# A hybrid attention layer on one core: keys and values projected second, the remaining projections run between attention units

## The chip, the cores and the metric

The kernel runs on one core of one Trainium2 chip. The metric is device time in microseconds (us) of one execution, the median over the runs. A core has TensorE (PE, matmuls into the PSUM banks; its weight loads are shown apart), VectorE (DVE), ScalarE (ACT), GpSimd (POOL) and SyncE (SP), which only issues DMAs here. Each engine works through its own instructions in order; semaphores tie them together.

## The reference

One layer of a backbone with 128 prompt tokens (tile t = 0) and 1024 latent tokens (t = 1 to 8), width 1024. All is fp32.

```
h = rmsnorm(x) * (1 + scale) + shift            # shift, scale, gate = silu(c) @ w_mod + b_mod
q_a k_a v_a g_a q_b k_b v_b g_b = split(h @ w_in)   # 8 query heads of 64, 2 key heads, for A and for B
q, k = rmsnorm per head; latent ones with 2-D axial rotation
A: softmax over all 1024 latent keys + 128 cached keys
B: softmax over keys with |i-j| <= 128 + 128 cached keys + a sink logit per head
y = x + gate * (concat(o_a * silu(g_a), o_b * silu(g_b)) @ w_out)
```

Prompt tokens attend to prompt keys alone. The outputs are y for both kinds of tokens, and the prompt's keys and values of A and B.

## The kernel before, in words

A product in fp32 is made of three matmuls: both operands are split into a high and a low part (fp32r), and high x high, high x low and low x high are added in PSUM. So the projection of one tile of 128 tokens onto 512 columns is 8 k-tiles x 3 = 24 matmuls of 512 columns (`project`, L247 to L251), and the gates, which are made transposed, are 24 matmuls a piece of 512, 256 or 384 columns (`gate_products`, L253 to L264). `Weights.split` makes the parts of one raw weight tile: a cast on ACT, a subtraction on DVE (for `gb`, every other one on POOL).

The program is one long list, written in the order in which each engine is to run it. `later(n, f)` puts work `n` ticks ahead; a tick comes every 12 projection matmuls, later once per attention slot. At the end `in_order` pins every engine to this order.

Before, the stages follow each other: modulation and mixer A's gates (W_GA), A's queries (W_QA, 9 tiles), B's queries (W_QB, 9 tiles), keys and values (W_KV, 9 tiles), B's gates (W_GB), then attention with the output projection.

- `query`: a projected query tile is squared on ACT, reduced on DVE, raised to -1/2 on POOL, scaled and rotated on DVE, transposed on TensorE, split into high (ACT) and low (DVE), and put into DRAM (`q_dram`). `u_load` brings it back for each unit.
- `key`: the same for keys, which stay in SBUF: `kha`, `kla` for A, `khb`, `klb` for B; values in `v_hi`, `v_lo`.
- A unit is (tile t, mixer m, key head g). An A unit has 9 key blocks, a B unit 3 or 4; a slot is one block. `scores` makes a block's scores in a B-bank; for A `exp` (L1123) and a cast (L1127) on ACT and a subtraction on POOL (L1131, the fifth block of a unit on DVE, L1129) give the high and low parts, for B the weights are normalised ahead and the block is a transpose, a cast (L1116) and a subtraction on DVE (L1117). `values` multiplies with the values LAG slots later (LAG = 3).
- Ahead of an A unit `max_items` makes row maxima (12 matmuls of 384 columns, L881, each with a reduction on DVE, L882), and a product into the tile `qb` (L901). Ahead of a B unit `weight_items` makes scores row by row (L938, L939), a masked reduction (L942), an exponential (L928) and the sums. Both use the two A-banks.
- At a unit's end `inverse`, `gated` and `parts` divide by the sums, multiply with the stored gates on POOL, and split into `ogh` (ACT, L1177) and `ogl` (POOL, L1179).
- `out_items`: 24 output matmuls (L1212) for each half of a tile go into `outq`; the slot loop takes OUTRATE of them per slot. `split_wo` splits the output weights in the places that the projections' inputs leave free.

Units alternate, A, B, A, B of each tile; the prompt's four units come last.

```
units = [(t, m, g) for t in range(1, NT) for g in range(2) for m in range(2)]
units[PROMPT_AT:PROMPT_AT] = [(0, m, g) for g in range(2) for m in range(2)]
```

The maxima of the first two A units are now made between B's gate matmuls (`EARLY`).

## Time and profile before

| | us |
|---|---|
| median of 3 runs (lowest to highest) | 711.58 (711.53 to 712.5) |
| profiled execution, first to last instruction | 709.6 |
| of it TensorE busy | 691.6 |
| DVE, ACT, POOL busy | 469.3, 409.9, 334.2 |

Stages by TensorE: gates of A done at 82.5, A's queries to 133.9, B's queries to 191.4, keys to 247.2, B's gates to 303.2, attention to 688.0, and the last output matmuls and sums to 709.6. The profiled execution's span stands 2.0 us under the median of the runs. TensorE's busy time is modelled for pipelined matmuls, so that two matmuls overlap in it; the distance between their starts tells more. A row of the groups gives line, engine, operation, output and input tiles, shapes, count, then busy us and mean ns of one, then the engine's idle time before them and what ended it.

### The profile page before, as it was taken

What the parts mean: (1) busy time and instruction counts of PE and PEld (TensorE: products, weight loads), DVE (VectorE), ACT (ScalarE), POOL (GpSimd) and SP (SyncE); (2) the same over time, 40 slices, a digit from 0 to 9 for tenths busy, and PEclk for the clock granted to TensorE, in tenths of its full rate; (3) what the DMA queues carried; (4) which work ended last, traced back from release to release, by engine and by line L of the source; (5) the groups of instructions that cost most, each with busy time, mean ns of one, the idle gap of its engine ahead of it and who ended that gap; (6) DMA issues with size and microseconds to landing.
All of it is one profiled execution on the core that took longest, in us unless ns stands there. A gap on an engine that the chain in (4) does not pass through costs nothing. (4 is left out here: it accounts for less than half of the span.)

```text
span 709.6 us, 10604 instructions
## 1 busy us (share of the span) xinstructions
PE 691.6 (97%) x3508; PEld 558.5 (79%) x3508; DVE 469.3 (66%) x1019; ACT 409.9 (58%) x829; POOL 334.2 (47%) x356
## 2 busy tenths in 40 slices
PE   7999999999999999989999999999999999999987
PEld 4778988878787889966788888888888888787865
DVE  4667257967848945647867578666775776675662
ACT  5646412412403431188777887787778777877760
POOL 3547023233213421256756655665576557555660
PEclk9999999999999999999999999999999999999999
DMA  8962283358353116332222121212221221222323
GB/s 316 415 211 102 78 302 74 90 154 263 84 139 104 37 39 215 123 108 57 78 68 85 50 82 53 71 57 75 68 82 38 79 71 50 78 72 70 104 67 121
DMA packets 53560, 78.58 MB, mean 111 GB/s; under 512 B 7096, under 2 KB 25720, under 8 KB 52608
## 3 DMA queue, kind: packets, MB, share of 16 engines
q1 hardware_dynamic: 45328, 65.96, 28.1%
q10 hardware_dynamic: 8176, 11.94, 6.3%
q8 instruction: 28, 0.46, 0.3%
q14 instruction: 28, 0.23, 0.1%
HBM read 58.69 MB, written 19.18 MB: 110 GB/s over the span
## 5 line engine op out<-in xcount | busy, mean ns | idle before, releaser
L1131 POOL TENSOR_TENSOR pl<-pe,ph 128x512 fp32r<-128x512 f32 x130 | 167.7, 1292 | 145.0 <-DVE nm L942 67.5
L882 DVE TENSOR_REDUCE mx<-pmx 128x1 f32<-128x384 f32 x192 | 101.4, 552 | 56.3 <-PE pmx L881 54.8
L1123 ACT ACTIVATE pe<-st 128x512 f32<-128x512 f32 x146 | 86.8, 594 | 28.2 <-PE st L1121 27.4
L1127 ACT CAST ph<-pe 128x512 fp32r<-128x512 f32 x146 | 90.6, 621 | 4.8
L1141 PE MATMUL pv<-ph,v_hi 128*128 128x512 f32 x208 | 82.8, 398 | 2.2 <-DVE spare L1165 2.2
L1144 PE MATMUL pv<-pl,v_hi 128*128 128x512 f32 x208 | 82.4, 396 | 0.0
L1212 PE MATMUL po<-wo,ogh 128*128 128x512 f32 x216 | 72.6, 395 | 0.2 <-DVE yt L1219 0.2
L174 POOL TENSOR_TENSOR rs_q<-ms_q,mhalf 128x8 f32<-128x8 f32 x18 | 34.1, 1896 | 80.9 <-DVE ms_q L172 80.9
L942 DVE CUSTOM_DVE_ANT_0 sn<-sn,mask,nsink 128x512 f32<-128x512 f32 (+1 forms) x64 | 46.4, 724 | 38.0 <-PE sn L939 37.6
L881 PE MATMUL pmx<-kha,qt 128*128 128x384 f32 x192 | 61.2, 363 | 0.4 <-ACT pen L928 0.2
L1120 PE MATMUL st<-qt,kha 128*128 128x512 f32 x144 | 58.2, 404 | 1.9 <-ACT pe L1123 1.1
L1121 PE MATMUL st<-qb,kla 68*128 68x512 f32 x144 | 57.5, 399 | 1.1 <-DVE qb L901 1.1
L1143 PE MATMUL pv<-ph,v_lo 128*64 128x512 f32 x146 | 57.6, 395 | 0.0
L1144 PEld LDWEIGHTS pv<-pl,v_hi 128*128 128x128 f32 x208 | 39.2, 189 | 16.4
L928 ACT ACTIVATE pen<-sn,nm 128x512 f32<-128x512 f32 (+2 forms) x72 | 45.0, 626 | 6.5 <-DVE nm L942 3.1
L1116 ACT CAST ph<-st 128x512 fp32r<-128x512 f32 x62 | 36.4, 587 | 19.9 <-PE st L1115 18.7
L1141 PEld LDWEIGHTS pv<-ph,v_hi 128*128 128x128 f32 x208 | 39.3, 189 | 10.6 <-ACT ogh L1177 2.4
L646 ACT CAST qo0q<-ptq 128x512 fp32r<-128x512 f32 x18 | 10.6, 586 | 60.7 <-PE ptq L643 55.8
L1212 PEld LDWEIGHTS po<-wo,ogh 128*128 128x128 f32 x216 | 40.0, 188 | 6.8 <-DVE yt L1219 0.6
L1117 DVE TENSOR_TENSOR pl<-st,ph 128x512 fp32r<-128x512 f32 x62 | 42.5, 686 | 2.7 <-ACT ph L1116 2.1
L1212 PE MATMUL po<-wo,ogl 128*128 128x512 f32 x108 | 42.6, 394 | 0.0
L881 PEld LDWEIGHTS pmx<-kha,qt 128*128 128x128 f32 x192 | 35.6, 191 | 6.4 <-DVE mx L882 1.3
(213 smaller groups left out, 1699.2 us busy)
## 6 DMA issues: line engine op xcount, KB each, us to landing
qt<-qd SPq DMA_DIRECT2D x36, 256.0 KB, 3.0
wm<-in_w_mod_ss_dram SPq DMA_DIRECT2D x7, 1024.0 KB, 10.0
qd<-qo0q ACTq DMA_DIRECT2D x36, 128.0 KB, 2.4
qd<-qo1q ACTq DMA_DIRECT2D x36, 128.0 KB, 2.4
sgl<-gd SPq DMA_DIRECT2D x36, 128.0 KB, 2.2
out_dram<-yt SPq DMA_DIRECT2D x17, 256.0 KB, 2.0
xn<-in_x_sample_dram SPq DMA_DIRECT2D x8, 512.0 KB, 7.2
wg<-in_w_mod_g_dram SPq DMA_DIRECT2D x4, 1024.0 KB, 8.3
```

The lines of the kernel that those rows point to most:

```text
L881: nc.tensor.matmul(pm[:, 0:384], lhs, kha[:, g, 3 * b : 3 * b + 3, :], start=True, stop=True)
L882: nc.vector.tensor_reduce(mx[:, h, b : b + 1], pm[:, 0:384], axis=AX.X, op=ALU.max)
L942: nc.vector.tensor_tensor_reduce(s, s, mask[:, m0 : m0 + n], -1.0, nsink[:, 4 * g + h : 4 * g + h + 1], op0=ALU.add, op1=ALU.min, accum_ou ...
L1120: nc.tensor.matmul(s, kh, qtile[i], start=True, stop=False)
L1121: nc.tensor.matmul(s, kl, qbtile[i], start=False, stop=True)
L1123: nc.scalar.activation(pe, s, AF.Exp)
L1127: nc.scalar.copy(ph, pe)
L1131: nc.gpsimd.tensor_tensor(pl, pe, ph, op=ALU.subtract)
L1141: nc.tensor.matmul(pv, two, ph, start=(b == 0), stop=False)
L1143: nc.tensor.matmul(pv[0:64, :], vl, ph, start=False, stop=False)
L1144: nc.tensor.matmul(pv, two, pl, start=False, stop=last)
L1212: nc.tensor.matmul(po[n], a, wo_parts[KT * n + k][lo], start=(k == KS[0] and p == 0), stop=(k == KS[-1] and p == 2))
```

## The change

The stages are put in another order. Behind A's gates come keys and values; behind them the first five tiles of A's queries; then attention begins. The other 13 query tiles and all of B's gates become a list `light` of single matmuls, which the slot loop takes from at LIGHT = 6 columns-of-512 per slot between a unit's own matmuls, while eleven A units run (t = 1 to 5, and the first of t = 6). B units and the output projection begin after them.

```
FIRST_UNITS = [(t, 0, g) for t in range(1, 6) for g in range(2)] + [(6, 0, 0)]
REST = """B1.0 B1.1 A6.1 B2.0 B2.1 A7.0 B3.0 B3.1 A7.1 B4.0 B4.1 A8.0 B5.0 B5.1 A8.1 B6.0 B6.1
 B7.0 B7.1 A0.0 A0.1 B8.0 B0.0 B0.1 B8.1"""
OUT_ORDER = (1, 2, 3, 4, 5, 6, 7, 0, 8)
```

To make room, B's keys and values are put into DRAM when they are made and loaded later, and the gated outputs of A units of t = 1 to 8 are put into DRAM and fetched, one half at a time, when their tile's output is due. Fewer buffers stand between the steps: LAG 3 to 2, NOG 5 to 4, PES 3 to 2, and one `desk` for the query steps. Query parts are put by SP instead of ACT once attention runs; B's gates are made without `Silu` (as x times exp(-ln(1 + exp(-x)))), so that ACT keeps its set of functions.

```diff
-LAG = 3
+LAG = 2
-NOG = 5
-PES = 3
+NOG = 4
+PES = 2
-OUTRATE = 2.5
-PADRATE = 3
+LIGHT = 6.0
+OUTRATE = 3.9
+SOON = 5
+MX_LEAD = 9
+NAT_LEAD = 7
...
+        order = list(range(1, NT)) + [0]
+        for m, (w, nxt) in enumerate(((W_QA, W_QB), (W_QB, W_GB))):
+            for t in order:
+                items = project_items(w, nxt, m, t, t == order[-1])
+                if t == order[-2]:
+                    items.insert(0, (0.0, nxt.load_all))
+                light += items
...
+        light.append((0.0, lambda: later(1 + QUERY_SLOT[-1] + 2, queries_done)))
+        for a, b in THIRDS:
+            for ch in range(4):
+                light += piece_items(W_GB, ch, slice(a, b), (lambda a=a: marks[a]()) if ch == 3 else None)
+        early = SOON * 24
+        while early:
+            tick()
+            for _ in range(12):
+                light.pop(0)[1]()
+                early -= 1
...
+    def queries_done():
+        qpool.close()
+        late_pools.append(ctx.enter_context(tc.tile_pool(name="b1", bufs=1, side="right")))
...
+        load_keys(b1, "hi", khb_dram)
+    def third_2():
...
+        later(3, finished)
+    def finished():
+        p1.close()
+        late_pools.append(ctx.enter_context(tc.tile_pool(name="b2", bufs=2, side="right")))
+        b2 = late_pools[1]
+        load_keys(b2, "lo", klb_dram)
+        kb["v"] = b2.tile([P, 20, 2, HD], F32R, name="v_b", bufs=1)
+        nc.sync.dma_start(kb["v"].bitcast(F32), vb_dram)
+        fetch(OUT_ORDER[0])
...
         def parts():
-            while held[0] == NOG:
...
+            if (t, m, g) in of_dram:
+                nc.sync.dma_start(of_dram[t, m, g], v["of"])
+            else:
+                split_out(t, 2 * m + g, v["of"])
+    def fetch(t):
+        def load(g):
+            ofl = late_pools[1].tile([P, 2, P], F32, tag="ofl", name=f"ofl{t}_{g}", bufs=1)
+            nc.sync.dma_start(ofl, of_dram[t, 0, g])
+            later(2, lambda: split_out(t, g, ofl))
+        for g in range(2):
+            if (t, 0, g) in of_dram:
+                later(1 + 4 * g, lambda g=g: load(g))
...
+    for n in range(12):
+        items[n]()
+        for _ in range(2):
+            light.pop(0)[1]()
...
     for s in range(len(slots) + LAG + PROMPT_END[3]):
         tick()
         if s < len(slots):
             live.append((slots[s], slots[s] and scores(slots[s][0], slots[s][1], slots[s][3])))
+        rate[0] = min(rate[0] + LIGHT, 8.0)
+        while light and rate[0] >= max(light[0][0], half):
+            n, f = light.pop(0)
+            rate[0] -= n
+            f()
...
+        credit = min(credit + OUTRATE, 7.0) if outq else 0.0
         while outq and credit >= 1.0:
             outq.pop(0)()
             credit -= 1.0
```

`third_0`, `third_1` and `third_2` run when a third of B's gates is done, and split the output weights into the places that come free. The slots number 212 as before: 0 to 98 are the eleven A units, 99 to 104 B's two units of t = 1, then the order of REST.

More of the change, by code (lines that the diff above doesn't have):

```diff
@@ L839, in hybrid_step @@
-        gb = gates(W_GB, 1, None, THIRDS)
-        later(1, lambda: sg_tile.append(lambda n: wrp.tile([P, 512], F32, tag="raw", name=n)))
-        mm_tags[0] = "BC"
-        for _ in range(4):
-            next(gb)
-    qs = ctx.enter_context(tc.tile_pool(name="qs", bufs=2, side="right"))
-    qs.tile([P, 8], F32, name="pad2", bufs=1)
-    qp = ctx.enter_context(tc.tile_pool(name="qp", bufs=2, side="right"))
-    units = [(t, m, g) for t in range(1, NT) for g in range(2) for m in range(2)]
-    units[PROMPT_AT:PROMPT_AT] = [(0, m, g) for g in range(2) for m in range(2)]
+            put_keys(k2, 0, "c")
@@ L1038, in split_wo @@
         (nc.gpsimd if i % 2 else nc.vector).tensor_tensor(lo, raw, hi, op=ALU.subtract)
-    mask = qp.tile([P, 512], BF16, name="mask", bufs=1)
-    mask32 = wrp.tile([P, 512], F32, tag="raw", name="mask32")
-    nc.sync.dma_start(mask32, k_mask)
-    later(2, lambda: nc.vector.tensor_copy(mask, mask32))
-    for i in range(LOADED):
-        u_load(i)
-    for i in EARLY:
-        items, end = max_items(i)
-        beside[2] += items + [end]
-    beside[:2] = 0.0, (len(beside[2]) + 0.5) / 64
-    def wo_step(i, *then):
-        split_wo(i)
@@ new lines, in set_ready, with pump @@
+    def set_ready(t, a):
+        ready.add((t, a))
+        pump()
+    parts_in_order = [(t, x) for t in OUT_ORDER for x in ("A", 2, 3)]
+    def pump():
+        while len(pushed) < len(parts_in_order):
+            t, x = parts_in_order[len(pushed)]
+            if not all((t, a) in ready for a in ((0, 1) if x == "A" else (x,))):
+                return
+            pushed.append((t, x))
+            outq.extend(out_items(t, range(4) if x == "A" else range(2 * x, 2 * x + 2)))
+            if x == 2:
+                fetch(OUT_ORDER[OUT_ORDER.index(t) + 1] if t != OUT_ORDER[-1] else None)
```

666 lines of the change are left out of this document (375 added, 291 removed).

## The prediction

> **What bounds the kernel now.** I read the page first, then busy time by stage, the chain, the order of TensorE's instructions, TensorE's waits, and last the durations on the other engines. The page, and a view of busy time in stretches (columns: stretch, its length, then busy time and instructions of PE, PE's weight loads, DVE, ACT and POOL, granted clock, DMA share, GB/s):
>
> ```profile
> span 709.6 us, 10604 instructions
> PE 691.6 (97%) x3508; PEld 558.5 (79%) x3508; DVE 469.3 (66%) x1019; ACT 409.9 (58%) x829; POOL 334.2 (47%) x356
> ```
>
> ```profile
> 133.90:191.40 57.50, 57.50 (x287) 44.82 (x285) 44.36 (x84) 14.80 (x27) 15.79 (x10) 1.00 0.57 161
> 191.40:247.20 55.80, 54.53 (x259) 44.54 (x258) 43.26 (x127) 17.69 (x45) 16.96 (x17) 1.00 0.33 86
> 247.20:303.20 56.00, 56.00 (x331) 51.77 (x329) 33.34 (x77) 9.82 (x24) 11.15 (x9) 1.00 0.39 128
> 303.20:340.40 37.20, 33.53 (x154) 23.93 (x153) 21.70 (x50) 32.61 (x69) 25.64 (x26) 1.00 0.29 82
> 340.40:673.70 333.30, 332.16 (x1605) 267.21 (x1605) 227.72 (x482) 261.59 (x525) 199.79 (x213) 1.00 0.22 70
> 65.90:82.50 16.60, 16.60 (x98) 16.60 (x97) 3.02 (x6) 7.04 (x14) 1.68 (x4) 1.00 0.31 116
> 17.74:35.50 17.76, 17.76 (x137) 13.27 (x137) 12.38 (x27) 12.14 (x24) 10.44 (x15) 1.00 1.03 415
> ```
>
> TensorE is the bound nearly everywhere, at full clock. A busy TensorE hides short waits, so I price its work by the distance between starts. The chain (start, length, what) gives that of a matmul over 512 columns, the timeline that of four transposes with one matmul over 384 columns:
>
> ```profile
> 688.03 5.48 PE po L1212 x24
> ...
> 695.01 9.85 PE po L1212 x42
> ```
>
> ```profile
> 316.50 0.60 PE L1115 MATMUL st<-ident_r,pen 128*128 128x128 f32 x4
> 316.85 0.42 PE L881 MATMUL pmx<-kha,qt 128*128 128x384 f32 x1
> 317.11 0.39 PE L1141 MATMUL pv<-ph,v_hi 128*128 128x512 f32 x1
> ```
>
> 512 columns: 5.48/24 = 0.228 and 9.85/42 = 0.235 us; I use 0.231. 384 columns: the stretch 65.90:82.50 is 96 of them (and two others) in 16.60 us, 0.173. Four transposes: 317.11 - 316.50 - 0.173 = 0.44.
>
> With these prices I count two stretches. The first 24 slots of attention (303.2 to 340.4, before output matmuls join) hold 96 matmuls of 512 columns, 33 of 384, six groups of transposes and 2 output matmuls: 22.2 + 5.7 + 2.6 + 0.5 + 0.2 for small ones = 31.2 us, but lasted 37.2. Its busiest other engine, ScalarE, was busy 32.6. Later a pair of units (A 45 matmuls and 12 maxima, B 16 and four groups of transposes, output 24) is 85 x 0.231 + 12 x 0.173 + 4 x 0.44 + 0.2 = 23.7 us; fourteen pairs are 332 us and took 333.3. So there is no loss as long as output matmuls fill the gaps, and 6.0 us where nothing fills them: such a stretch lasts about 1.14 times its busiest other engine (37.2/32.6).
>
> What TensorE waited for after the projections (total, times, longest):
>
> ```profile
> PE pv L1141 <- DVE spare L1165: 2.2, 4, 0.9
> PE ptk L745 <- DVE klp L763: 1.2, 1, 1.2
> PE st L1121 <- DVE qb L901: 1.1, 2, 0.6
> ```
>
> **The change, part by part.** TensorE's instructions stay the same in kind and number: every projection, maximum, score, value and output matmul is issued once, in another order. So the sum is the span, less what TensorE loses now, plus what it will lose. The profiled execution (span 709.6) stands 2.0 below the median of the runs, 711.58; I add 2.0 at the end.
>
> What goes. Attention starts with projections as filler: -6.0. Keys are projected right behind the A gates instead of behind B's queries, whose work DVE still had queued: the wait of 1.2 goes. The waits at the end and for qb (2.2 and 1.1) go with their places; new ones are counted below. That leaves 709.6 - 10.5 = 699.1.
>
> What comes is worked out with these durations (columns: line, engine, operation, shape, count, busy us, mean ns, idle before):
>
> ```profile
> L882 DVE TENSOR_REDUCE mx<-pmx 128x1 f32<-128x384 f32 x192 | 101.4, 552 | 56.3 <-PE pmx L881 54.8
> L1117 DVE TENSOR_TENSOR pl<-st,ph 128x512 fp32r<-128x512 f32 x62 | 42.5, 686 | 2.7 <-ACT ph L1116 2.1
> L942 DVE CUSTOM_DVE_ANT_0 sn<-sn,mask,nsink 128x512 f32<-128x512 f32 x48 | 36.4, 758 | 27.1 <-PE sn L939 26.9 <-ACT pen L928 0.2
> L236 DVE TENSOR_TENSOR wlokv<-rawkv,whikv 128x512 fp32r<-128x512 f32 x8 | 5.0, 682 | 0.0
> L236 DVE TENSOR_TENSOR wlogb<-rawgb,whigb 128x512 fp32r<-128x512 f32 x4 | 3.8, 979 | 1.3 <-ACT whigb L234 1.3
> ...
> L1127 ACT CAST ph<-pe 128x512 fp32r<-128x512 f32 x146 | 90.6, 621 | 4.8
> L1123 ACT ACTIVATE pe<-st 128x512 f32<-128x512 f32 x146 | 86.8, 594 | 28.2 <-PE st L1121 27.4
> L1116 ACT CAST ph<-st 128x512 fp32r<-128x512 f32 x62 | 36.4, 587 | 19.9 <-PE st L1115 18.7 <-POOL ogl L1179 0.9
> L928 ACT ACTIVATE pen<-sn,nm 128x512 f32<-128x512 f32 x48 | 32.9, 686 | 3.9 <-DVE nm L942 3.1
> L928 ACT ACTIVATION_READ_ACCUMULATOR pen<-sn,nm 128x1 f32 x72 | 13.9, 193 | 0.0
> L1156 ACT ACTIVATE rs<-rs 64x512 f32<-64x512 f32 x18 | 11.4, 632 | 0.6
> L1177 ACT CAST ogh<-spare 128x256 fp32r<-128x256 f32 x36 | 14.4, 402 | 1.5 <-POOL spare L1167 1.5
> ...
> L1131 POOL TENSOR_TENSOR pl<-pe,ph 128x512 fp32r<-128x512 f32 x130 | 167.7, 1292 | 145.0 <-DVE nm L942 67.5 <-ACT ph L1127 57.4 <-POOL pl L1131 11.2
> L1179 POOL TENSOR_TENSOR ogl<-spare,ogh 128x256 fp32r<-128x256 f32 x36 | 26.5, 738 | 0.0
> L1038 POOL TENSOR_TENSOR wo<-wraw,wo 128x512 fp32r<-128x512 f32 x6 | 7.7, 1288 | 39.4 <-DVE wo L1037 26.0 <-PE pg L259 5.8 <-PE pmx L881 4.7
> ```
>
> A query tile's normalising and rotation, from 133.90:191.40 (nine tiles and eight weight splits): DVE (44.36 - 8 x 0.682)/9 = 4.3 us, ScalarE (14.80 - 8 x 0.62)/9 = 1.1, POOL 15.79/9 = 1.75.
>
> 1. Keys into A's queries. Eight weight splits with four raw tiles loaded ahead; DVE works 43.26/9 = 4.8 us a key tile (191.40:247.20) against TensorE's 24 x 0.231 = 5.5, and behind the same boundary, into B's gates, TensorE is now busy for all of 247.20:303.20. 0.5 (0 to 2).
>
> 2. Opening of attention. Unit 0's twelve maxima run with 24 projection matmuls, then 12 more: to slot 0's second score matmul TensorE has about 11.5 us (2.1 + 8.2 + transposes 0.9 + 0.2). On DVE the same span holds twelve maxima (6.6), pieces of four queries (about 7) and the product into qb (0.7): 14.3, and DVE's order is fixed. The difference is 2.8. I take 3 (1 to 5: half of the query pieces late, or a scale waiting for POOL's power on top).
>
> 3. Slots 0 to 81, A units with filler. The filler is 18 x 24 matmuls of queries, less 120 before and 36 in the opening, is 276; B's gates add 4 x 24 x (1 + 0.5 + 0.75) = 216. At six a slot 492 last 82 slots. A slot is 5 x 0.231 + 6 x 0.228 + 1.33 x 0.173 = 2.8 us for TensorE, against ScalarE 0.594 + 0.621 + 1.1/4 = 1.5, POOL 1.15 + 1.75/4 = 1.6, DVE 0.74 + 0.08 + 4.3/4 = 1.9. The lag between scores and values falls from three slots to two, 5.6 us, over a chain of 0.594 + 0.621 + 1.292 = 2.5. Weight splits come in bursts of eight, in which ScalarE stands in order behind raw tiles still loading. 1 (0 to 4). The high B keys (1.57 MB of new traffic, at the 415 GB/s of the stretch 17.74:35.50 3.8 us) go down SP's queue at slot 51, and the next unit's qb load stands behind them with three slots, 8.4 us, in hand: 0 (0 to 2).
>
> 4. Slots 82 to 92: filler used up, no output matmuls yet. Eleven A slots: TensorE 55 x 0.231 + 12 x 0.173 = 14.9 with the small ones. ScalarE: 11 x 1.215, the last gates' three passes (1.5), two unit ends (2 x 1.23), two output casts (0.8) = 18.1. POOL: ten subtractions (12.9), three of the output weights' splits (3.9), three products of 0.74 = 19.0. POOL sets this stretch: 19.0 x 1 to 1.14 = 19.0 to 21.7, a loss of 4.1 to 6.8, of which the next six slots (POOL 7.6 against TensorE 15.7) can take back some 1.5. Behind it stands a queue: at slot 84 SP sends the low B keys and B's values (2.88 MB, 6.9 us at 415 GB/s) ahead of A's first stored output, and ScalarE's cast of that output (slot 87) would block the exponentials behind it. 4.5 (2.6 to 8).
>
> 5. Slots 99 to 108: both B units of t=1 and four A slots, output empty again after its first 24. TensorE 12.5; ScalarE 13.5 (six casts of 0.587, four A slots, four to five exponentials of 0.88, unit ends, output casts). 13.5 x 1 to 1.14: 1.0 to 2.9 over. 1.5 (1 to 3).
>
> 6. Four cycles of B, B, A (17 slots): TensorE 125 x 0.231 + 12 x 0.173 + 8 x 0.44 + 0.3 = 34.8, ScalarE 27.5, the 79% it has now (261.59 of 333.30). But 48 output matmuls at 3.9 a slot leave five slots dry, and the lag is two. Slots 130 to 134 are the worst: DVE 12.5 (eight score reductions of two B units, 0.758 each, subtractions 0.686, output sums) against TensorE 10.8. Between nothing (fourteen pairs lose nothing now) and 1.5 a cycle: 1 (0 to 6).
>
> 7. Slots 182 to 201, four B units in a row, weights only four slots ahead: TensorE 36.8, DVE 34.9, ScalarE 33.7. 1 (0 to 3).
>
> 8. The end. The last tile's A halves are fetched one after the other through one buffer, the second only after POOL has taken the first: POOL 0.738, the load, ScalarE 0.402, POOL 0.738, with the load by these rows:
>
> ```profile
> qt<-qd SPq DMA_DIRECT2D x36, 256.0 KB, 3.0
> ...
> sgl<-gd SPq DMA_DIRECT2D x36, 128.0 KB, 2.2
> ```
>
> about 4.5 with handovers against some 14 matmuls, 3.2 us, then 48 output matmuls (11.1). 2 (0.5 to 4).
>
> Sum: 0.5 + 3 + 1 + 4.5 + 1.5 + 1 + 1 + 2 = 14.5; 699.1 + 14.5 = 713.6; with 2.0, 715.6.
>
> A row that speaks against mixing: the same subtraction on DVE takes 979 ns where POOL runs its twin (wlogb) and 682 where POOL does not (wlokv). [...]
>
> **The rivals.** First, faster: the lag of two slots covers what POOL and ScalarE run over in parts 4 to 7, as it covers the dry slots of a pair now, and the following filler takes all of it back. Then part 4 costs 1 and parts 5 to 7 nothing: 14.5 - 7.0 = 7.5 and 708.6. For it: 333.3 against 332. Against it: 37.2 against 31.2, with a lag of three. It decides once all new losses stay under 9.1.
>
> Second, DVE becomes the bound in slots 0 to 48. All two-input work beside POOL's subtractions at 979/682 = 1.44 times: 2.2 us of each query's 4.3 and 16 splits add some 16 us to the 110 counted there (49 x 1.9, 16 splits, unit ends), 126 against TensorE's 140; in the bursts of slots 7 to 10 DVE (12.8) already passes TensorE (11.3). About 5 more: 720.6.
>
> Third, no net change: losses equal gains, 10.5 against 10.5, 711.6. TensorE was full before and after, so that the change does no more than move its waits.
>
> Fourth, everything hidden: ScalarE's attention and TensorE's projections fit beside each other all the way, and the removal stands with nothing given back, 699.1 + 2.0 = 701.1. For it the 2.8 us slot of part 3; against it that filler ends at slot 82 of 212. [...]
>
> **How the numbers follow.** Forecast (713 to 719) 0.37; second rival and the upper ends of parts 2 and 4 (719 to 724) 0.11; no change 0.14; first rival (704 to 710) 0.31; fourth 0.07. A measurement here can tell about 0.2%, 1.4 us, from no change. Faster 0.38, same 0.14, slower 0.48. The range 703 to 721 leaves out the fourth rival and the upper end; the forecast's own is 712 to 719.
>
> **What would show it.** Right: the slices around slot 82 to 92 show TensorE short of work and POOL or ScalarE at nine tenths; the wait of st for qb at slot 0; TensorE's waits between 0 and 81 near zero; a gap before the last 42 output matmuls. Wrong: if TensorE's matmuls keep 0.231 us through the dry slots (first rival), or if the lit slots last over 2.9 us (second), or if ScalarE stands behind the stored output for more than 6 us.

## The result, and the profile after

The changed kernel takes 822.27 us (median of 4 runs, 821.22 to 828.76) against 712.04 for the kernel before beside it: 1.157 times as long, with a 95% interval of 1.1525 to 1.1612. The forecast was 715.6. The direction was right, and the size was off by 107 us; with slower at 0.48 and a forecast of 4 us, the direction was luck. The profiled execution spans 821.0 us. Its page (first lines, and the granted clock in 40 slices):

```profile
span 821.0 us, 10859 instructions
PE 733.3 (89%) x3508; PEld 570.9 (70%) x3508; DVE 501.4 (61%) x1042; ACT 421.2 (51%) x862; POOL 337.2 (41%) x356
PEclk9999999898899999999999998999999999999799
```

TensorE still runs 3508 matmuls, but is busy for 89% of the span instead of 97%, and its clock is no longer full throughout. Its busy time itself grew by 41.7 us for the same matmuls. In the 58.0 us of the span at half clock it was busy for 46.9, with matmuls that the prediction's prices put at 24.3, so that the clock lengthened them by some 23 us (an estimate from the trace and those prices). The other 19 us of growth stand at full clock and were not taken apart. No other engine comes near to full. Busy time by stage (columns as in the prediction's view of stretches):

```profile
138.80:184.70 45.90, 35.31 (x148) 26.55 (x149) 32.31 (x84) 11.20 (x26) 9.24 (x6) 0.93 0.32 92
184.70:204.60 19.90, 14.25 (x58) 10.82 (x58) 12.95 (x26) 3.45 (x5) 1.64 (x1) 0.83 0.20 47
204.60:265.50 60.90, 51.23 (x205) 39.73 (x204) 42.08 (x74) 28.67 (x49) 25.18 (x19) 0.89 0.40 112
265.50:327.90 62.40, 58.26 (x265) 45.33 (x264) 45.60 (x79) 32.35 (x54) 32.58 (x25) 1.00 0.26 68
398.30:475.30 77.00, 77.00 (x414) 67.14 (x413) 47.52 (x92) 48.74 (x87) 40.26 (x33) 1.00 0.28 89
475.30:504.40 29.10, 19.23 (x69) 12.32 (x68) 16.10 (x27) 16.46 (x30) 17.26 (x15) 0.82 0.62 218
557.30:717.50 160.20, 147.76 (x692) 112.97 (x691) 96.27 (x207) 99.91 (x216) 68.28 (x84) 1.00 0.24 76
```

Of these rows only 398.30:475.30, where the filler is B's gates, has no loss. In the first three rows DVE has the most to do beside TensorE, and is busy for 65 to 70% of them. TensorE's waits (total, times, longest; some rows left out):

```profile
PE pmx L951 <- DVE mx L952: 20.1, 18, 2.9
PE pmx L951 <- DVE desk L649: 7.2, 3, 3.3
PE ptq L638 <- DVE desk L628: 6.5, 4, 2.2
PE st L1206 <- ACT pe L1209: 5.0, 1, 5.0
PE sn L1021 <- DMA qt<-qd: 3.2, 1, 3.2
PE st L1207 <- DMA qb<-qd: 2.8, 1, 2.8
PE pq L844 <- ACT whiqa L233: 2.7, 1, 2.7
```

They are many, and most end with DVE: `mx` is the maxima's reduction, `desk` are a query's steps (L628 adds the rotation, L649 makes the low part). The chain at the change from A's to B's query weights (start, length, what) shows how DVE can be late and yet not busy:

```profile
229.86 0.61 ACT desk L610
230.49 0.70 DVE ssq L612
231.46 1.65 POOL rs_q L173
233.14 0.70 DVE desk L617
...
237.43 0.70 DVE wloqb L235
238.15 2.57 DMA rawqb<-in_w_in_dram
...
245.03 2.80 DMA rawqb<-in_w_in_dram
247.91 0.63 ACT whiqb L233
248.56 0.69 DVE wloqb L235
249.25 0.61 DVE ssq L612
250.05 0.59 DVE tcos L573
250.65 0.61 DVE tsin L573
251.25 0.48 DVE mx L952
251.77 0.69 PE pmx L951
```

Query steps wait for POOL's power, splits wait for a raw tile that is loaded only after an earlier one is split, and the maximum that TensorE needs stands behind all of them in DVE's fixed order.

To place the loss, the trace's starts of score matmuls are set against a count of TensorE's work alone, slot by slot, at the prediction's prices (together 695 us; the prediction came to 699.1 from the other side, by taking off losses). The count is an estimate, and it does not hold for the slots of e9_queries_first, which have less filler. Columns: start of slot 0, then lengths of slots 0-19, 20-39, 40-48, 49-59, 60-81, 82-98, 99-113, 114-181, 182 to the end; last, time of the span at half clock.

| profiled kernel | slot 0 | 0-19 | 20-39 | 40-48 | 49-59 | 60-81 | 82-98 | 99-113 | 114-181 | 182-end | half |
|---|---|---|---|---|---|---|---|---|---|---|---|
| counted, no loss | 183 | 56.7 | 57.7 | 25.7 | 31.0 | 60.9 | 30.6 | 25.3 | 139.3 | 85 | |
| changed | 204.6 | 76.3 | 62.4 | 34.7 | 35.7 | 61.6 | 49.2 | 32.9 | 160.1 | 103.5 | 58 |
| e1_fetch_first | 205.1 | 75.4 | 62.4 | 34.9 | 35.8 | 61.6 | 47.1 | 33.1 | 161.3 | 103.8 | 56 |
| e2_two_pairs | 203.9 | 74.9 | 62.4 | 35.1 | 35.8 | 61.6 | 49.2 | 32.9 | 159.9 | 103.8 | 50 |
| e3_keep_busy | 206.8 | 79.6 | 62.4 | 32.5 | 38.3 | 61.6 | 49.4 | 33.0 | 159.8 | 103.7 | 46 |
| e4_in_pieces | 205.2 | 76.7 | 62.4 | 34.6 | 31.1 | 61.6 | 46.9 | 33.0 | 160.5 | 105.2 | 60 |
| e6_apart | 204.2 | 79.6 | 62.4 | 35.2 | 34.7 | 61.6 | 47.4 | 33.3 | 154.0 | 104.0 | 77 |
| e7_more_raw | 202.7 | 73.2 | 62.4 | 29.7 | 33.9 | 61.6 | 49.5 | 33.4 | 160.1 | 105.0 | 46 |
| e9_queries_first | 333.5 | 46.6 | 46.0 | 17.8 | 24.7 | 55.9 | 37.8 | 33.0 | 161.7 | 105.0 | 104 |
| e11_query_spread | 197.1 | 75.7 | 60.7 | 34.2 | 32.7 | 61.6 | 50.0 | 32.9 | 161.9 | 103.5 | 61 |
| e13_same_weights | 202.7 | 70.3 | 62.4 | 26.7 | 35.0 | 61.6 | 49.8 | 32.9 | 159.9 | 106.2 | 49 |
| e12_together | 203.4 | 66.4 | 60.7 | 31.5 | 32.8 | 61.6 | 43.0 | 32.8 | 153.5 | 104.6 | 53 |
| f1_sp_later | 203.2 | 66.4 | 60.7 | 31.6 | 32.8 | 61.6 | 43.3 | 32.8 | 148.4 | 98.1 | 45 |
| f2_loaded | 200.7 | 66.4 | 60.8 | 32.7 | 32.7 | 61.6 | 44.0 | 33.3 | 152.5 | 105.0 | 59 |
| f3_both | 201.0 | 66.3 | 60.7 | 32.7 | 32.8 | 61.6 | 43.9 | 33.3 | 148.6 | 97.9 | 48 |
| f4_seven_weights | 202.6 | 66.4 | 60.7 | 32.8 | 32.8 | 61.6 | 39.2 | 31.8 | 152.1 | 105.3 | 49 |
| g1_longer_head | 203.6 | 68.7 | 60.5 | 35.4 | 31.0 | 59.6 | 41.2 | 33.7 | 148.4 | 97.3 | 45 |
| g2_pool_product | 202.4 | 65.2 | 63.4 | 31.1 | 32.8 | 61.6 | 44.3 | 32.3 | 148.4 | 98.1 | 45 |

The opening (up to slot 19) differs by some 3 us between executions in which nothing there was edited (e6_apart); the other columns repeat within about 1, the last within 2 to 3.

### The profile page after: what moved, and what is told of

Its sections match the earlier page's. It is cut to its first block, busy times and chain, and to the rows that moved or that the text cites. A ratio compares the mean times of both kernels' runs of the same rounds, so it can differ in the third digit from the quotient of the medians.

```text
span 821.0 us, 10859 instructions
## 1 busy us (share of the span) xinstructions
PE 733.3 (89%) x3508; PEld 570.9 (70%) x3508; DVE 501.4 (61%) x1042; ACT 421.2 (51%) x862; POOL 337.2 (41%) x356
## 3 DMA queue, kind: packets, MB, share of 16 engines
q1 hardware_dynamic: 63360, 87.46, 33.3%
## 4 chain that ended last, share of the span: by engine, by line
PE 56%; DVE 18%; DMA 11%; ACT 5%; POOL 4%; issue 4%; SPq 1%; ACTq 0%; POOLq 0%; DVEq 0%
PE po L1334 11%; PE pq L844 6%; PE pg L869 5%; PE pv L1228 4%; PE pv L1225 4%; PE pmx L951 4%; PE st L1207 3%; PE st L1206 3%; PE pv L1227 3%; DVE mx L952 3%; PE st L1201 3%; POOL rs_q L173 2%; PE sn L1008 2%; DVE desk L564 2%; DMA vbd<-vb 2%
## 5 line engine op out<-in xcount | busy, mean ns | idle before, releaser
L1214 POOL TENSOR_TENSOR pl<-pe,ph 128x512 fp32r<-128x512 f32 x130 | 171.3, 1320 | 162.8 <-ACT ph L1210 122.4
L951 PE MATMUL pmx<-kha,qt 128*128 128x384 f32 x192 | 72.0, 387 | 34.3 <-DVE mx L952 20.1
L1012 DVE CUSTOM_DVE_ANT_0 sn<-sn,mask,nsink 128x512 f32<-128x512 f32 (+1 forms) x64 | 46.3, 725 | 79.6 <-PE sn L1009 75.1
L951 PEld LDWEIGHTS pmx<-kha,qt 128*128 128x128 f32 x192 | 37.1, 198 | 55.9 <-DVE mx L952 28.3
L1228 PE MATMUL pv<-pl,v_a 128*128 128x512 f32 x146 | 59.1, 405 | 2.3 <-POOL pl L1214 2.3
L1225 PE MATMUL pv<-ph,v_a 128*128 128x512 f32 x146 | 58.9, 404 | 0.0
L1227 PE MATMUL pv<-ph,v_a 128*64 128x512 f32 x146 | 58.4, 400 | 0.0
L844 PE MATMUL pq<-whiqa,h 128*128 128x512 f32 x144 | 53.9, 432 | 2.7 <-ACT whiqa L233 2.7
L869 PE MATMUL pg<-h,whigb 128*128 128x512 f32 (+2 forms) x192 | 54.5, 345 | 0.0
L844 PE MATMUL pq<-whiqb,h 128*128 128x512 f32 x144 | 52.2, 403 | 0.0
L173 POOL TENSOR_TENSOR rs_q<-ms_q,mhalf 128x8 f32<-128x8 f32 x18 | 30.2, 1678 | 52.8 <-DVE ms_q L171 49.5
L1251 POOL TENSOR_TENSOR side<-side,sgl 128x256 f32<-128x256 f32 x36 | 27.4, 762 | 42.0 <-DVE side L1249 28.6
## 6 DMA issues: line engine op xcount, KB each, us to landing
xn<-in_x_sample_dram SPq DMA_DIRECT2D x8, 512.0 KB, 10.4
```

The source lines that it names most:

```text
L844: nc.tensor.matmul(v["pq"], h_at(a, i, k, tok), b[k], start=(k == 0 and p == 0), stop=(k == KT - 1 and p == 2))
L869: nc.tensor.matmul(v["pg"], a[k][:, cs], h_at(b, i, k, to), start=(k == 0 and p == 0), stop=(k == KT - 1 and p == 2))
L951: nc.tensor.matmul(pm[:, 0:384], lhs, kha[:, g, 3 * b : 3 * b + 3, :], start=True, stop=True)
L1214: nc.gpsimd.tensor_tensor(pl, pe, ph, op=ALU.subtract)
L1225: nc.tensor.matmul(pv, two, ph, start=(b == 0), stop=False)
L1227: nc.tensor.matmul(pv[0:64, :], v_a[:, j, 2, :], ph, start=False, stop=False)
```

## The experiments

Times are medians with the ratio to the kernel before beside it; the changed kernel's ratio is 1.157.

### One wait at a time

e1_fetch_first:

```diff
+        fetch(OUT_ORDER[0])
-        load_keys(b2, "lo", klb_dram)
+        later(2, lambda: load_keys(b2, "lo", klb_dram))
-        nc.sync.dma_start(kb["v"].bitcast(F32), vb_dram)
-        fetch(OUT_ORDER[0])
+        later(6, load_values)      # kb["v"] = ..., its load
```

> Changed kernel, with the first stored A output fetched ahead of the low B keys and B's values (these go down SP's queue two and six slots later). Theory, the queue holds the fetch: ScalarE's wait of 8.8 us in the output cast of slot 87 goes, and with it TensorE's wait of 5.0 for it, part of the 2.55 before it and the half-speed slots behind it; 822 falls by 6 to 10, to 812 to 816. Rival, POOL and ScalarE set the pace of slots 82 to 92 in any case (19.0 to 21.7 us of POOL by my own sum) or B's score matmuls now wait for the later keys: 819 to 823.

822.53 us, ratio 1.1552 (1.1532 to 1.1573): the rival. ScalarE's cast in the changed kernel's timeline, and behind it the longest DMA pieces of the two chains near 490 us, changed kernel first, then the edited one:

```profile
495.20 0.41 ACT L1273 CAST ogh<-ofl 128x256 fp32r<-128x256 f32 x1 [8.82 <-DMA ofl<-ofd]
```

```profile
489.38 7.39 DMA spare<-in_w_out_dram
```

```profile
490.31 5.96 DMA qb<-qd
```

ScalarE's wait in that cast falls to 1.5 us, but the next small load on the queue is now late, and TensorE waits 4.0 us for it. Slots 82 to 98 gave 2.1 us. So the 2.88 MB of reloads delayed what stood behind them, whichever load that was.

e2_two_pairs:

```diff
             qo = [desk[:, 5 + i].bitcast(F32R) for i in range(2)]
+            if late[0] and turn_:
+                qo = [qx[1][:, i].bitcast(F32R) for i in range(2)]   # [P, 2, 512], closed at queries_done
```

> Changed kernel, with a second pair of output buffers for the turned queries during attention, so that ScalarE's copy of one query does not wait until the put of the query before has landed. Theory, the single pair holds ScalarE, then VectorE's subtraction, then the maxima and so TensorE: ScalarE's waits for the put (9.7 us in 204 to 266) go and the loss of 38.7 us in slots 0 to 81 falls by 10 to 18, to 804 to 812. Rival, the waits come from bursts of weight splits and the fixed order of VectorE: 818 to 825.

822.09 us, ratio 1.1546 (1.1521 to 1.1571): the rival. In the changed kernel ScalarE waited here between 204 and 266 us:

```profile
ACT desk L641 <- DMA qd<-desk: 9.7, 2, 5.2
```

With two pairs this row is gone, and ScalarE waits for TensorE's transposes of the queries instead (the row below, and 4.5 us more for the other pair):

```profile
ACT qx L643 <- PE ptq L638: 5.5, 1, 5.5
```

Slots 0 to 19 are 1.4 us shorter, no more than executions differ there.

### The clock

e3_keep_busy, in front of ten places of the order:

```diff
+        KEEP = {0: 9, 120: 8, 122: 12, 160: 8, 166: 6, 210: 8, 222: 10, 426: 6, 431: 9, 480: 10}
+            for _ in range(KEEP.get(done_mms[0], 0)):
+                nc.tensor.matmul(out, zero_r, ident_r.unsqueeze(1).to_broadcast([P, 4, P]), start=first, stop=first)
```

> Changed kernel, with 86 matmuls of a zero matrix (19.9 us in all, added to sums that are open anyway) put in front of the ten places before slot 60 where TensorE waited 1.6 to 3.3 us. No wait is removed; TensorE is only kept at work in them. Theory, the halved clock behind each wait costs time of its own: the half-speed windows between 142 and 398 us go, at TensorE's busy share in them 16.7 us, so 803 to 812. Rival, in the half-speed windows the other engines set the pace: no gain, and what the added matmuls are not covered by waits comes on top, 820 to 832.

829.74 us, ratio 1.1642 (1.1612 to 1.1672): the rival on the whole. Half-speed time fell from 58 to 46 us only, since the waits moved. But at one place the test can be read, slots 40 to 48, where no window at half speed is left, changed kernel first:

```profile
343.30:377.90 34.60, 30.17 (x124) 22.97 (x123) 23.26 (x37) 18.55 (x32) 20.80 (x16) 0.90 0.31 88
```

```profile
348.90:381.40 32.50, 30.44 (x141) 23.93 (x139) 23.14 (x37) 18.55 (x32) 20.94 (x16) 1.00 0.32 94
```

At full clock 17 more matmuls took 2.1 us less. In slots 0 to 9 and 49 to 59, with the added matmuls, 3.8 and 2.6 us more passed (the first little more than executions differ by there), and half-speed windows remained. So the clock adds to the waits in places. What it costs this kernel in all stays unmeasured: the 23 us above are what it lengthened, and in e10_three_waits a halved window in attention cost 1.1 us, of which half was made up, against 1.44 and 1.81 among B's gates.

e10_three_waits puts known waits into the kernel before, ahead of three groups of B's gate matmuls:

```diff
+            if m and ts.start == 0 and ch:
+                nc.tensor.matmul(pg[:, 0:64], ident_r, ident_r[:, 0:64], start=True, stop=True)
+                nc.scalar.copy(held_up, pg[:, 0:64])
+                for _ in range((0, 4, 10, 17)[ch]):
+                    nc.scalar.copy(held_up, held_up)
+                nc.tensor.matmul(pg[:, 0:64], ident_r, held_up, start=True, stop=True)
```

> The kernel before, with three waits put ahead of three groups of B's gate matmuls, a stretch in which TensorE was busy all the time: TensorE waits for a chain of 5, 11 and 18 short ScalarE copies, some 1.2, 2.4 and 3.8 us. Theory, a wait long enough to leave a clock window of 3.41 us more than half idle halves the granted clock for the next window, and where TensorE is the bound that costs about 1.7 us on top of the wait: the time grows by the waits plus 1.7 for one or two of them, 720 to 723. Rival, the clock plays no part: the waits alone, 718 to 720.

726.16 us (two runs) against 713.0, 13.2 more; ratio 1.0189 (1.0158 to 1.022). The waits, and windows of 3.41 us (third column from the right: granted clock):

```profile
PE pg L312 <- ACT held_up L311: 9.6, 3, 5.0
```

```profile
260.32:263.73 3.41, 0.46 (x3) 0.20 (x2) 0.00 (x0) 2.53 (x11) 0.00 (x0) 1.00 0.00 0
263.73:267.14 3.41, 3.23 (x10) 2.80 (x11) 0.75 (x2) 1.27 (x4) 0.00 (x0) 0.50 0.02 5
267.15:270.56 3.41, 3.41 (x16) 2.81 (x15) 0.00 (x0) 0.00 (x0) 0.00 (x0) 1.00 0.20 77
270.56:273.97 3.41, 1.14 (x6) 0.75 (x5) 0.00 (x0) 1.93 (x9) 0.00 (x0) 1.00 0.00 0
273.97:277.38 3.41, 0.64 (x3) 0.64 (x4) 0.00 (x0) 2.44 (x10) 0.00 (x0) 0.50 0.00 0
277.39:280.80 3.41, 3.41 (x11) 2.81 (x10) 0.75 (x2) 1.15 (x3) 0.00 (x0) 0.50 0.20 74
```

Above both ranges, since the waits came out longer than expected, 9.6 us in place of some 7.4; with 9.6 the rival comes to 722.6 and the theory to 724.3 to 726.0, so it is the theory. The time grew by 3.6 us more than the waits. By the starts of the same matmuls in both traces, the halved windows at 263.73 and 277.39 us, with 10 and 11 matmuls instead of 16, put TensorE back by 1.44 and 1.81 us, and a third, at 321.76 in attention, by 1.1, of which half was made up right behind it. The shortest wait (1.4 us) left the clock alone.

### Mixing, bursts and loads

e9_queries_first:

```diff
-SOON = 5
+SOON = 18
-LIGHT = 6.0
+LIGHT = 2.4
```

> Changed kernel, with all eighteen query projections ahead of attention (as filler remain only B's gates, 2.4 a slot in place of 6.0). Theory, it is the queries' work in attention that stalls TensorE (slots 0 to 48 lost 34 of the 38.7 us, the gates' slots almost none): projections run at 5.5 us a tile, attention's first 82 slots at about 2.0 us, and the loss between 139 and 475 us falls from about 60 to 10 to 20: 775 to 790. Rival, A's own chain with two slots of lag and short buffers stalls whatever the filler is, the more so with less filler: 810 or more.

864.53 us, ratio 1.2142 (1.2121 to 1.2163). Neither theory foresaw where: attention begins at 333.5 us. The early queries themselves are slow, as a stretch of them and DVE's longest waits among them show:

```profile
250.00:300.00 50.00, 37.49 (x146) 29.07 (x144) 23.58 (x46) 6.51 (x11) 8.19 (x5) 0.86 0.25 57
```

```profile
DVE ssq L612 <- ACT desk L610: 36.1, 13, 3.4
DVE desk L617 <- POOL rs_q L173: 27.8, 16, 1.8
```

146 matmuls in 50 us, against 287 in 57.5 in the kernel before (the prediction's row 133.90:191.40). The kernel before had its steps further apart, QUERY_AT (0, 2, 3, 6) in place of (0, 1, 2, 4); the change put them on one shared `desk` as well. Attention begins 128.9 us later and slots 0 to 81 take 79.7 us less. Of the difference, 16.9 us are one wait ahead of the first maximum, which the trace puts down to no engine. The same projections thus cost more ahead of attention than among it, so that mixing alone is not what makes them dear. Both rows above are steps of a query's own chain; that it is the chain was read from them, not tested.

e11_query_spread sets the steps apart:

```diff
-QUERY_AT = (0, 1, 2, 4)
+QUERY_AT = (0, 2, 3, 6)
-QUERY_SLOT = (0, 1, 2, 3)
+QUERY_SLOT = (0, 2, 3, 5)
```

> Changed kernel, with the steps of a query further apart (square; scale two slots later in place of one; turn five in place of three; the same in the half tiles before attention). Theory, a query's chain (ScalarE 0.60, VectorE 0.68 and 0.17, POOL's power 1.65) is longer than a slot, so that VectorE, whose order is fixed, waits in the scale for POOL with the maxima behind it: head and slots 0 to 49 (lost about 43 us) give 8 to 15, 807 to 814. Rival, the waits are those of the weight changes and the opening: 818 to 824.

813.35 us, ratio 1.1418 (1.1388 to 1.1447): the theory's mechanism, near its upper end. (Ahead of attention a query's place on `desk` is overwritten before it is turned, so part of y is other than the reference's; the instructions are the same.) Attention begins 7.5 us earlier, slots 20 to 39 give 1.7 and slots 49 to 59 give 3.0. In e12_together, whose steps ahead of attention overwrite nothing early, attention begins only 1.2 us earlier, so that most of the 7.5 us cannot be had this way.

e7_more_raw:

```diff
+    for w in (W_QB, W_GB):
+        w.pools[WRAW : WRAW + 2] = [(qx[1], 2)] * 2      # a pool closed at queries_done
```

> Changed kernel, with five raw weight tiles in place of three for the two weight changes inside attention. Theory, at a change of weights VectorE and ScalarE stand in order behind raw tiles that are loaded only when the tile before is split (loads of 2.6 and 2.8 us stand in the chain near 238 and 245 us): slots 9 to 16 and 43 to 50, which lost about 9 us each, give 3 to 5 each, 812 to 816. Rival, the burst of eight splits among the query's steps on VectorE is what costs, loaded or not: 819 to 823.

815.35 us, ratio 1.1446 (1.1411 to 1.1481): the theory. Slots 0 to 19 give 3.1 (no more than executions differ there), 40 to 48 give 5.0. The loads in sequence are a part.

e13_same_weights, the whole burst:

```diff
+            if self.tag in ("qb", "gb"):
+                self.hi, self.lo = W_QA.hi, W_QA.lo
+                return
```

> Changed kernel without the two weight changes in attention: B's queries and gates are projected with A's query weights, so that no raw tile is loaded and no weight is split after the first slot (the outputs are other than the reference's); all matmuls stay. Theory, the bursts of eight splits, their loads and what stands behind them in VectorE's and ScalarE's order cost 8 to 10 us each: 800 to 806. Rival, the query's own steps fill VectorE's order at these places and the bursts ride along: 815 to 821.

809.08 us, ratio 1.1353 (1.1324 to 1.1382), between the two: slots 0 to 19 and 40 to 48 give 14.0 together, of which the loads were 8.1 by e7. With no weight change at all, slots 0 to 19 still lose 14 us.

e4_in_pieces:

```diff
-        nc.sync.dma_start(kb[n].bitcast(F32), src)
+        for j, (g, p) in enumerate(((0, 0), (1, 0), (0, 6), (1, 6))):
+            later(1 + j, lambda g=g, p=p: nc.sync.dma_start(kb[n][:, g, p : p + 6].bitcast(F32), src[:, g, p : p + 6]))
```

and B's values the same way from the sixth slot on, behind the fetch.

> Changed kernel, with the three reloads for B (high keys, low keys, values; 4.5 MB) cut into four pieces each, one piece a slot, the stored A output fetched ahead of B's values. With the fetch alone moved, the stretch of slots 82 to 93 fell by 2 us only, because the product into qb then waited 6 us for its own load behind the keys. Theory, a lump on SP's queue delays whatever small load comes next, whichever it is: the wait of 2.8 for qb near 392 us and those of 5.0 to 6.0 near 490 go, slots 49 to 55 and 82 to 93 give 8 to 12 us, 809 to 814. Rival, POOL, DVE and the output weights' own loads set the pace there: 818 to 823.

815.79 us, ratio 1.1441 (1.1404 to 1.1478), between the two: slots 49 to 59 give 4.6, so that they are at the count, and 82 to 98 give 2.3. The lump of B's high keys cost 4.6 us where it fell; in e11_query_spread, which sends it whole two slots later, the wait for qb is gone too and these slots give 3.0. B's other reloads give little more than they did in e1.

### Where two kinds of work meet

e6_apart:

```diff
-            at, end = [start[i] - MX_LEAD + a for a in MX_AT], start[i] - MX_LEAD + MX_END
+            lead = MX_LEAD - (i >= len(FIRST_UNITS))
+            at, end = [start[i] - lead + a for a in MX_AT], start[i] - lead + MX_END
-            at0 = start[i] - NAT_LEAD
+            at0 = start[i] - NAT_LEAD - (i < 26)
```

> Changed kernel, with B's score matmuls one slot earlier and A's maxima one slot later from slot 99 on, so that they no longer fall into the same slots. Now slots 113, 114, 130, 131, 147 and 148, in which they coincide, last 4.1 to 5.4 us against 1.7 to 2.4 for their neighbours. Theory, both take turns at two PSUM banks and at one engine that reduces them, and a score bank stays taken until ScalarE's exponential a slot later: cycles give 2.5 to 3.5 us each, slots 96 to 98 some 2, 806 to 812. Rival, the work on VectorE is the same and only moves into other slots: 819 to 823.

816.74 us, ratio 1.147 (1.1411 to 1.1528). Slots 130 and 131 fall from 5.39 and 4.58 us to 3.29 and 2.41; the cycles give 6.1 together, 82 to 98 1.8. TensorE's waits in the cycles (557 to 717 us of the changed kernel, then 555 to 711 of the edited one, whose first such row is now another):

```profile
PE pmx L951 <- DVE mx L952: 6.8, 7, 1.1
```

```profile
PE pti L1060 <- DVE mx L952: 2.9, 4, 1.2
```

Between the two: the theory's mechanism, with half of its gain.

e5_before_short, on the kernel before: LAG 2, PES 2, NOG 4.

> The kernel before, with the changed kernel's shorter buffers alone: two slots between scores and values in place of three, two exponential tiles in place of three, four output pairs in place of five. Theory, the short buffers are what the later cycles lose by (21 us over the count in slots 114 to 182 of the changed kernel): the long stretch of unit pairs, 333.3 us now, grows by 10 to 20, 722 to 733. Rival, output matmuls as filler cover it and the loss of the cycles is where score reductions and maxima meet: 711 to 715.

720.05 us, ratio 1.0113 (1.0085 to 1.014), 7.0 us more, between the two. By the starts of score matmuls, blocks 24 to 200 grew by only 2.3 (324.9 before). The rest stands in the first 24 (1.8) and behind block 200 (3.5). Short buffers cost little while output matmuls stand as filler in every slot, and 7 of the changed kernel's 110 us would be their part if it were the same there, which was not tried.

### Edits together

e12_together is e4, e6, e7 and QUERY_SLOT of e11, with QUERY_AT = (0, 2, 3, 4).

> Changed kernel, with four edits at once: B's reloads in pieces, B's scores and A's maxima apart, five raw weight tiles, and a query's steps further apart (before attention only as far as no tile is overwritten too early). Alone they gave 4.6 us in slots 49 to 60 and 2.3 in 82 to 93, 7 in slots 114 to 148, 9 in slots 0 to 60, and 4 to 8 around the opening. Theory, each takes away a loss of its own place and the gains add up: 794 to 801. Rival, VectorE's fixed order lets a wait removed in one place come back in the next: 806 to 814.

791.82 us, ratio 1.11 (1.1067 to 1.1134), 30.5 us less: the theory, a little under its range. The gains of separate places add up.

f1_sp_later adds to it:

```diff
-                    nc.sync.dma_start(y_tile[t][...], yt[n][:, q])
+                    later(2, store)                                   # the same store
-            nc.sync.dma_start(rd, iv)
+            later(1, lambda: nc.sync.dma_start(rd, iv))
-            later(GATE_LATE, lambda: load_gate(i + GATES))
+            later(GATE_LATE + (i < 26), lambda: load_gate(i + GATES))
-                nc.sync.dma_start(of_dram[t, m, g], v["of"])
+                later(1, lambda: nc.sync.dma_start(of_dram[t, m, g], v["of"]))
```

> The kernel of the four edits (791.8 us), with SP's issues moved to where their data is there: y's stores two slots later, the stores of A's outputs and of the row sums one, the gate loads one. Theory, SP stands in order behind issues that wait (67 us behind y's sums, 56 behind the gates' buffers, 51 behind the row sums) and the loads behind them land late (the query load that TensorE waits 3.2 us for near 757, with half speed after it): slots 182 to the end and the cycles give 5 to 12, 780 to 787. Rival, the loads come early enough but for that one: 789 to 793.

780.67 us, ratio 1.0967 (1.0941 to 1.0993): the theory. SP's waits behind y's sums, and TensorE's for the late query load, in e12_together and then what is left in f1_sp_later, where the second has no row:

```profile
SPq L1350 <- DVE spare L1349: 58.8, 15, 11.4
...
PE sn L1025 <- DMA qt<-qd: 3.7, 1, 3.7
```

```profile
SPq L1353 <- DVE spare L1351: 18.8, 11, 7.1
```

The cycles give 5.1 us and slots 182 to the end 6.5.

f2_loaded loads A's eight raw query tiles at once:

```diff
-                W_QA.load_all()
+                for j in range(2):
+                    raw = kt.tile([P, 4, 512], F32, tag="wg", name=f"raw_qa{j}", bufs=2)
+                    nc.sync.dma_start(raw, w_in[512 * j : 512 * j + 512, CQ[0] : CQ[0] + 512]...)
...
```

> The kernel of the four edits, with all eight raw tiles of A's query weights loaded ahead, in the place of the gate weights that are used up by then. Theory, at the boundary from keys to A's queries the raw tiles are loaded one behind the other after their splits (2.7 and 2.9 us stand in the chain), VectorE is late from there on and the opening with it: 4 to 8 us, 784 to 788. Rival, VectorE is behind with the key tiles' own steps, and the loads are covered by them: 789 to 793.

790.25 us, ratio 1.1097 (1.1069 to 1.1125): the rival. Attention begins 2.7 us earlier; the chain there is now DVE's key steps, splits and query steps one behind the other.

> The kernel of the four edits with the two edits of f1_sp_later and f2_loaded together. If losses of separate places add up: the sum of what the two give, 774 to 784. If one covers the other: as the better of the two.

779.41 us, ratio 1.0946 (1.0916 to 1.0975): the sum, of which f2's part cannot be told from nothing.

f4_seven_weights leaves out nine of the sixteen output weights' loads and splits:

```diff
+        if i > 6:
+            wo_parts[i] = wo_parts[i % 7]
+            return
```

> The kernel of the four edits without the loads and splits of nine of the sixteen output weight tiles (the first seven are used in their place; the outputs are other than the reference's); the matmuls stay. Theory, between the end of the filler and the first output matmuls these nine splits on VectorE and POOL, and their loads, hold up the subtractions and maxima: of the 20 us that slots 82 to 114 lose, 8 to 12 go, 780 to 784. Rival, ScalarE's two passes a slot and POOL's subtraction of 1.3 us set the pace with no filler in TensorE: 788 to 792.

786.61 us, ratio 1.1049 (1.1025 to 1.1073), 5 us less: slots 82 to 113 give 4.8 of some 20 over the count. Between the two.

g1_longer_head and g2_pool_product, on f3_both:

```diff
-        for _ in range(2):
+        for _ in range(4):
             light.pop(0)[1]()
-        if n == 5:
+        if n % 2 == 1:
```

> The kernel of the six edits, with 48 projection matmuls between unit 0's twelve maxima in place of 24 (taken from the slots behind). Theory, in the opening VectorE's backlog of query steps stands ahead of the maxima and TensorE lacks work: the waits of 1.8, 2.1 and 4.2 us in front of slot 0 go, 772 to 777. Rival, the added projections bring their own steps to VectorE just as early, and TensorE waits for them a little later: 778 to 783.

781.42 us, ratio 1.0974 (1.0957 to 1.099): the rival. The wait of 4.2 us in front of slot 0 is gone, and slots 0 to 19 and 40 to 48 grow by 2.4 and 2.7.

```diff
-        nc.vector.tensor_tensor(ra, qn, cb, op=ALU.mult)
+        (nc.gpsimd if places else nc.vector).tensor_tensor(ra, qn, cb, op=ALU.mult)
```

> The kernel of the six edits, with the first of a query's three rotation products on POOL in place of VectorE (0.69 us off VectorE's order, about 1.3 on POOL's, and one handover more). Theory, VectorE's steps in their order set the pace from the boundary to slot 20 and at the weight changes: 18 x 0.7, of which the part in those places counts, 3 to 8 us, 771 to 776. Rival, a query's own chain sets it, and that grows by 0.6 and the handover: 780 to 790.

781.77 us, ratio 1.0989 (1.0964 to 1.1015): the rival's range, with no gain. But the edit did not take work off DVE. The two other products, which now run beside POOL's, take twice as long, f3_both first, then the edited one (stretch 138 to 400 us):

```profile
L564 DVE TENSOR_TENSOR desk<-desk,tsin 128x256 f32<-128x256 f32 x32 | 15.3, 519 | 0.0
```

```profile
L564 DVE TENSOR_TENSOR desk<-desk,tsin 128x256 f32<-128x256 f32 x32 | 31.8, 1035 | 0.5
```

Over the span DVE is busy for 507.1 us in place of 500.6. So the run does not show whether less work on DVE would help.

## Why the prediction was wrong, step by step

TensorE's prices were right as far as the runs tell: slots 60 to 81 took 61.6 us against 60.9 counted, and the instructions are the same 3508. What went, 10.5, cannot be read apart from what came. What came, 14.5, was wrong in every term. Against the prediction's 699.1 the trace has some 122 us more, against the count of 695 some 126, which the parts below add up to.

- **Part 1** (0.5, bounds 0 to 2): about 13 up to 184.7. Taking B's gates as the model for this boundary failed: A's raw tiles came one by one and DVE had key and query steps behind each other; f2 gave 2.7 of it, e11 7.5 together with the opening, e12 with the steps that overwrite nothing 1.2.
- **Part 2** (3): 8.6, above its upper end of 5.
- **Part 3** (1, bounds 0 to 4) is the step that failed most: 38.7. It set busy times per slot against TensorE's 2.8 and found every engine below it. That holds in the trace (42.08 of 60.90 us on DVE) and says nothing of the order. As the chain shows, a query's steps, one slot apart, need some 3.1 us to the power's end (0.60 + 0.70 + 0.18 + 1.65) in slots of 2.8, and the maxima stand behind them. What the runs took back of the 38.7: steps set apart 5.8 (e11), both weight changes left out 14 (e13), so that the term for "bursts of eight", at most 4 with all the rest, was the most undersized; query steps, raw tiles and key reload together 17.7 (e12). The cause of the other half stays open. The khb load, priced at 0 (0 to 2), cost 4.6: the three slots in hand for the qb load behind it were too few.
- **Part 4** (4.5, up to 8): 14.3, and 4.3 in the six slots behind, which were to take 1.5 back. The place and the queue behind the stored output were right (ScalarE stood for 8.8 us, over the 6 named as a sign). That removing it would give this back was not said, and e1 shows that it does not.
- **Part 6** (1, bounds 0 to 6): 21. Slots 130 to 134 were rightly named the worst (16.3 us), but priced by DVE's sum, 12.5 against 10.8. Of the 21, 6.1 went with reductions of both kinds no longer taking turns at two A-banks (e6), and 5.1 with SP's issues no longer behind waiting ones (f1); the rest stays open.
- **Parts 5, 7 and 8** (1.5, 1 and 2): about 7.5 (4.1 of it in slots 99 to 108), 7.9 and 10.4. Of part 7, 3.2 us are TensorE's wait for a query load near 757 us, with half speed behind it. Of part 8, the gap before the last output matmuls is there, 1.8 us behind the fetched half's cast; the rest was not taken apart.
- **At full clock**, in the first part, was assumed for the changed kernel too. 58 us of it ran at half speed. The prediction had no term for that.

Of the rivals, none was right. The second named the right slots and the right sign (slots 0 to 48 last 3.5 us each, over its 2.9), and priced them at 5 us. Its premise is in the trace: DVE's products of two SBUF tiles take longer, kernel before first, then the changed one:

```profile
L557 DVE TENSOR_TENSOR ra_q<-qnq,tcos 128x512 f32<-128x512 f32 x16 | 11.1, 693 | 0.5
```

```profile
L559 DVE TENSOR_TENSOR desk<-desk,tcos 128x512 f32<-128x512 f32 x16 | 14.4, 897 | 0.5
```

In the changed kernel up to 400 us, those of them that overlap an instruction of POOL take 1.06 us on average (nine), the others 0.69 (seven). For the products of half the width it is 0.88 against 0.42, for their sum 0.92 against 0.68, while steps with an input in PSUM (L617) stay at 0.69. Together with B's query weights (902 ns a split, 681 before) DVE is busy for 13.5 us more by such rows, near the rival's 16. What that is worth to TensorE no run takes apart. The fourth and its ground, that ScalarE's attention and TensorE's projections fit beside each other, fails at the same step as part 3: they fit by busy time. More raw tiles gave 5.0 us in slots 40 to 48 (e7); a second pair of output buffers (e2) and raw tiles loaded ahead (f2) gave next to nothing.

Still open is most of what f3_both keeps, 68 us more than the kernel before. By the table it loses, over the count, some 18 up to slot 0, 10 in slots 0 to 19, 12 in 20 to 59, 21 in 82 to 113, 9 in the cycles and 13 behind slot 182. Not tried were two things that the traces show: a query's products kept off POOL's subtractions, and SP's longest wait, 102.0 us in f3_both, of the query puts behind ScalarE's copies, with the loads of weights and units behind them. No run here shows a version that beats the kernel before.

## What to carry to other kernels

When stages are mixed, busy time per stage bounds the gain but not the loss: follow one item's chain through the engines in their fixed order, and compare the time between two of its steps on the same engine with the time that the order leaves between them, before counting shares. Take durations beside the work that they will be mixed with, too: the same product took 0.69 us alone and 1.06 beside POOL (changed kernel, L559). Removing the wait that a view names may give next to nothing where another stands right behind it (e1, e2, g1), while setting the steps further apart, cutting a lump of DMA into pieces and issuing a store when its data is there each paid in its place, and their gains added up. A DMA issue that waits can hold the loads behind it on its queue: with SP's issues moved to where their data is there (f1_sp_later), TensorE's wait of 3.7 us for a query load went, and the kernel took 780.67 us in place of 791.82.

## What the runs showed of the hardware that was not expected

In the trace of the changed kernel the granted clock falls from 1.00 to 0.50 eleven times, for 58.0 us in all. Each of these spells begins a multiple of 3.41 us after the first, at 142.26 us; seven last 3.41 us, two 6.83 and two 10.24. In the 3.41 us ahead of the eleven, TensorE was busy for 0.42 to 1.77 us. Cut into stretches of 3.41 us from 142.26 both ways, the trace has, behind its first 15 us, eleven full-speed stretches in which TensorE was busy for less than half: ten stand ahead of half speed, and one does not (1.49 us busy, 162.74 to 166.15). The one other spell, at 217.36, follows 1.77 us of work. Six half-speed stretches, with 0.73 to 3.04 us of work, were followed by half speed again, and the last ones of the eleven spells have 3.09 to 3.41 us of work. Ahead of four spells stands a single wait of TensorE in such a stretch, 2.2, 2.2, 2.9 and 1.8 us long (near 207, 238, 249 and 357 us). These are counts of one execution. In e10_three_waits two halved stretches among B's gates, where TensorE is the bound, cost 1.44 and 1.81 us.
